# Moving weight and activation tiles by multiples of 32 bytes in a float32 decoder trunk

## The chip, the cores and the metric

The kernel runs on one core of a Trainium2 chip. The metric is device time in microseconds (us), lower is better. A core has five engines that run side by side, each with its own instruction queue: TensorE (PE; the load of its stationary operand is listed apart as PEld), VectorE (DVE), ScalarE (ACT), GpSimd (POOL) and SyncE (SP), which here only starts transfers. Two things are read by TensorE out of the on-chip memory (SBUF) at the same time: the **moving** operand of the matmul that runs, and the **stationary** operand ("weights" in the profile, LDWEIGHTS) of the matmul that comes next.

## The reference

A batch of one, 256 positions, width 2048, two layers, everything in float32:

```python
for l in range(DEPTH):                      # 2
    h = rms_norm(x, norm1_g[l])
    z = h @ w_in[l]                         # 2048 x 5120
    q, k, v, gu, gv = split(z)              # 1024 columns each
    attn = dilated_attention(rotary(q), rotary(k), v)
    gm = chunked_gmlp(gelu(gu), gelu(gv), ...)
    x = x + concat(attn, gm) @ w_out[l]     # 2048 x 2048
    h2 = rms_norm(x, norm2_g[l])
    x = x + square(relu(h2 @ w_up[l])) @ w_down[l]   # 2048 x 8192, 8192 x 2048
return rms_norm(x, final_g)
```

Nearly all the work is the four products with a weight matrix.

## The kernel before

**Float32 out of three products.** Every weight element and every activation is split into a high part (rounded to the type float32r, in which a matmul runs in one pass) and a low part (the rest). A product is then three matmuls: weight high by activation high, weight low by activation high, weight high by activation low.

**Weight steps.** The weights are cut into 736 blocks of 128 x 1024 elements (`Sub`), 512 KB each, in the order of use. One *step* is the work on one block: SP loads it into a buffer `raw` (L106), ACT copies it rounded into `hi` (`high`, L113), DVE subtracts into `lo` (`low`, L121), and PE runs the matmuls. The three tiles come from rings of buffers, `raw` 6, `hi` 7, `lo` 6; a ring's next buffer is free when its last readers are done. The number of the step (`self.i`) fixes the buffer.

**Two kinds of step.** In a `transposed` step (672 of 736) the weight block is the stationary operand: for each of two column blocks and four row blocks there are three matmuls of 128 x 256, one each on L263 (weight high), L265 (weight low) and L267 (weight high), so 24 in a step, with the activation as the moving operand. That is `hs`, the normed input, in 352 of the steps (q, k, gu and the MLP's up product); in the other 320 it is a tile `half` (1024 features, high and low; `new_half`), which holds the attention's output, the gating's output, or one eighth of the MLP's inner activations: two for `w_out` (`mix_a`, `mix_g`), eight for `w_down` (`hid[e]`), each layer. There are two `half` buffers, used in turn. In a `natural` step (64: v and gv) the activation `hs` is stationary and the weight block moves: 12 matmuls of 128 x 512, on L286 (high), L287 (low), L288 (high).

**Order.** The program is written out by one loop over the steps. At step `done` it emits `high` up to six blocks ahead, `low` up to five ahead, then the loads as far as the `raw` ring allows, then the matmuls; small pieces of attention and gating are put between the steps by a list with due times. In the MLP 16 up steps (one eighth) and 16 down steps take turns.

```python
ahead = min(2 + max(done - 10, 0) // 2, LO_BUFS - 2)
high_to(done + 2 + ahead)
low_to(done + 1 + ahead)
load_to(n_low[0] + RAW_BUFS)
mm()
```

**Where the tiles lie.** Tiles are laid one after another in each partition of SBUF, in units of 32 bytes. `hs` begins at a multiple of 64 bytes, and so does every 256-column piece of it. Behind it stands `warm`, one element, which takes 32 bytes; `raw`, `hi` and `lo` follow (4,096 bytes each), further on `half` (16,384 bytes each). All of these therefore begin 32 bytes past a multiple of 64, and so does each 128-column piece that a matmul reads of them. Below, a start is called *even* (a multiple of 64) or *odd* (32 past one).

Of the kernel before, what the change touches and what calls it, by code (L numbers as in the profile page):

```python
# [22 lines left out]
F32R = mybir.dt.float32r  # L23
# [5 lines left out]
P = 128  # L29
D = 2048  # L30
S = 256
DEPTH = 2
KC = D // P
NH = 8
# [9 lines left out]
BRANCHES = ((128, 1), (512, 4), (2048, 16))  # L44
NEG = -1.0e30

RAW_BUFS = 6
HI_BUFS = 7
LO_BUFS = 6
BUDGET = 1.2  # L50
# [22 lines left out]
def trunk(ctx: ExitStack, tc: tile.TileContext, layout, xT, consts, gains, w, b_sp, w_sp, out):  # L73
# [3 lines left out]
    wp = ctx.enter_context(tc.tile_pool(name="wp", bufs=1))  # L77
    tp = ctx.enter_context(tc.tile_pool(name="tp", bufs=1))
# [5 lines left out]
    def t32(name, shape, bufs=1, tag=None):  # L84
        return tp.tile([P, *shape], F32, name=name, tag=tag or name, bufs=bufs)
# [8 lines left out]
    class Sub:  # L94
# [7 lines left out]
        def load(self, parts):  # L102
            self.raw = wp.tile([P, 1024], F32, name="raw", tag="raw", bufs=RAW_BUFS)
            m = 1024 // parts
            for j in range(parts):
                nc.sync.dma_start(self.raw[:, j * m:(j + 1) * m], w[self.i][:, j * m:(j + 1) * m])  # L106

        def high(self, parts):
            self.h = wp.tile([P, 1024], F32R, name="hi", tag="hi", bufs=HI_BUFS)
            self.hi = self.h.rearrange("p (k n) -> p k n", n=self.n)  # L110
            m = 1024 // parts
            for j in range(parts):
                act.activation(self.h[:, j * m:(j + 1) * m], self.raw[:, j * m:(j + 1) * m], AF.Copy)  # L113

        def low(self, parts):
            lo = wp.tile([P, 1024], F32R, name="lo", tag="lo", bufs=LO_BUFS)
            self.lo = lo.rearrange("p (k n) -> p k n", n=self.n)
            m = 1024 // parts
            for j in range(parts):
                r = slice(j * m, (j + 1) * m)  # L120
                vec.tensor_tensor(lo[:, r], self.raw[:, r], self.h[:, r].bitcast(F32), op=OP.subtract)  # L121
# [176 lines left out]
    def from_tiles(tiles, n):  # L298
        return lambda k: tiles[k // n][0][:, k % n, :, :]

    def new_half(cell):
        cell[0] = tp.tile([P, NH, 2, S], F32R, name="half", tag="half", bufs=2)

    def gelu(z, u, then):

# [12 lines left out]
    def pair(ps):  # L318
        return ps.rearrange("p (a b) -> p a b", a=2)

    def update(norm, c, ps, final, last):

        alone = last and c == KC - 2
        for j in range(2) if alone else [slice(0, 2)]:
            xj = x[:, c + j, :] if alone else x[:, c:c + 2, :]
            vec.tensor_tensor(xj, xj, pair(ps)[:, j, :], op=OP.add)  # L326
        if final:
            if not last:
                norm.chunks(c)
            norm.square(c, alone)  # L330
            if last:
                norm.gain(c)

    def layer(l, n1, n2, n3, last):
# [104 lines left out]
        def values(j, pts):  # L439
            ps = aux_bank()  # L440
            vt = par["vt"]
            for h in range(2):
                c = (2 * j + h) * P
                pe.matmul(ps[:, h * S:(h + 1) * S], lhsT=vt[:, 0, c:c + P], rhs=pts[h][:, 0:S], start=(h == 0),  # L444
                          stop=False, skip_group_check=True)
                pe.matmul(ps[:, h * S + P:(h + 1) * S], lhsT=vt[:, 1, c:c + P], rhs=pts[h][:, S:3 * P], start=False,  # L446
                          stop=True, skip_group_check=True)
            if mix_a[0] is None:
                new_half(mix_a)
            to_half(mix_a[0], 2 * j, ps.rearrange("p (a b) -> p a b", a=2))  # L450
            par["heads"] += 1

        def to_half(t, c, src):
            act.activation(t[:, c:c + 2, 0, :], src, AF.Copy)  # L454
            vec.tensor_tensor(t[:, c:c + 2, 1, :], src, t[:, c:c + 2, 0, :].bitcast(F32), op=OP.subtract)  # L455
# [61 lines left out]
        def gate(g0, u, ps):  # L517
            sp = t32("sp", [2, S], tag="cross", bufs=2)
            for h in range(2):
                g = g0 + h  # L520
                vec.scalar_tensor_tensor(sp[:, h, :].rearrange("p (a b) -> p a b", a=2),
                                         ps[:, h * S:(h + 1) * S].rearrange("p (a b) -> p a b", a=2),
                                         lnb[:, l, 0, g:g + 1],
                                         par["spb"][:, g, None, :].to_broadcast([P, 2, P]),
                                         op0=OP.mult, op1=OP.add)
            vec.tensor_tensor(u, u, sp, op=OP.mult)
            if mix_g[0] is None:
                new_half(mix_g)
            to_half(mix_g[0], g0, u)
# [21 lines left out]
        hid = [[None] for _ in range(8)]  # L551

        def after_up(e):
            def f(c, ps):
                if hid[e][0] is None:
                    new_half(hid[e])
                z = t32("mz", [2, S], tag="tmpA")
                vec.tensor_tensor(z, pair(ps), n2.R[:, None, :].to_broadcast([P, 2, S]), op=OP.mult)  # L558
                vec.scalar_tensor_tensor(z, z, 0.0, z, op0=OP.max, op1=OP.mult)  # L559
                to_half(hid[e][0], c // P, z)  # L560
            return f

        base = len(steps)
        for e in range(9):
            if e < 8:
                transposed("w_up", l, 0, KC, e * 1024, 1024, from_hs, after_up(e))
            if e:
                transposed("w_down", l, (e - 1) * 1024, 8, 0, D, from_tiles([hid[e - 1]], NH),
                           lambda c, ps, e=e: update(n3, c // P, ps, e == 8, last))
# [19 lines left out]
    def load_to(n, parts=1):  # L589
        while n_load[0] < min(n, len(subs)):  # L590
            c = 2 * n_load[0]
            if c < KC:
                nc.sync.dma_start(x[:, c:c + 2, :], xv[:, c:c + 2, :])
            subs[n_load[0]].load(parts)
            n_load[0] += 1
# [6 lines left out]
    def low_to(n, parts=1):  # L602
        while n_low[0] < min(n, len(subs)):
            subs[n_low[0]].low(parts)
            n_low[0] += 1
# [4 lines left out]
    act.activation(warm, ones[:, 0:1], AF.Tanh)  # L610
    for i in range(RAW_BUFS):
        load_to(i + 1, 2 if i == 0 else 1)
# [6 lines left out]
    for n, (wt, mm, after) in enumerate(steps):  # L619
# [3 lines left out]
        else:  # L623
# [5 lines left out]
# [3 lines that stand above are left out]
# [9 lines left out]
    n = norms[-1]  # L641
# [42 lines left out]
```

## Time and profile before

| | |
|---|---|
| median of 2 runs | 2117.82 us (2117.58 to 2118.06) |
| profiled execution | 2117.06 us, of which the span of instructions is 2115.0 us |
| granted TensorE clock | 0.997 of full speed |
| PE / DVE / ACT / POOL busy | 2097.5 / 1254.7 / 929.9 / 63.2 us |
| transfers | 395.36 MB, mean 187 GB/s |
| an up step (moving `hs`) against a down step (moving `half`) | 340 against 355 matmuls touch a stretch of 40 us |

A group's row gives line, engine, operation, the tiles written and read, their shape and the count, then busy time and the mean time of one. A matmul's own time (about 280 ns) is longer than the distance from its start to the next one's (about 115 ns), since the array works on several in a row; what the span is made of is the distance between starts. In the order rows below, a name in brackets after "waits" is a counter that the instruction waits for: DMAHW of a transfer, DVE or Activation of those engines.

### The profile page before, as it was taken

The page shows a single profiled execution, that of the slowest core. Times are in us where ns is not written, and L with a number is a line of the kernel's source. Part 1 is how long each engine was busy: PE and PEld are TensorE (multiplying, and loading weights), DVE is VectorE, ACT ScalarE, POOL GpSimd, SP SyncE. Part 2 cuts the span into 40 slices and gives each one's busy share as a digit, 9 for nine tenths or more (in the row PEclk, how much of TensorE's full clock was granted, in tenths as well). Part 3 has the DMA queues.
Part 4 walks back from the last instruction along what each step waited for, and adds up shares of the span by engine and source line. Part 5 has one row for each costly group of instructions (what it writes and reads, how often), then busy time and mean ns, then how long its engine had stood idle before and what let it go on. Part 6 is the DMA issues. An engine that isn't in the chain of part 4 may idle for free.

```text
span 2115.0 us, 40168 instructions
## 1 busy us (share of the span) xinstructions
PE 2097.5 (99%) x17212; PEld 2057.2 (97%) x17212; DVE 1254.7 (59%) x1502; ACT 929.9 (44%) x1128; POOL 63.2 (3%) x90
## 2 busy tenths in 40 slices
PE   8999999999999999999999999999999999999997
PEld 7998999999999999999989989999999999999997
DVE  7566766555555555555755666665565555555555
ACT  6555444344333433433545554543443334434333
POOL 0002300000000000000000032000000000000000
PEclk9999999999999999999999999999999999999998
DMA  8545555555555556556564455555655655555552
GB/s 306 183 160 169 180 192 180 196 192 178 189 200 188 192 180 200 191 183 198 188 211 157 164 180 176 195 177 198 200 180 180 199 191 200 181 187 192 182 201 84
DMA packets 111523, 395.36 MB, mean 187 GB/s; under 512 B 12272, under 2 KB 16368, under 8 KB 111344
## 3 DMA queue, kind: packets, MB, share of 16 engines
q1 hardware_dynamic: 110480, 390.12, 54.7%
q8 instruction: 134, 2.20, 0.4%
q10 hardware_dynamic: 864, 2.68, 0.3%
q14 instruction: 45, 0.37, 0.1%
HBM read 390.65 MB, written 2.10 MB: 186 GB/s over the span
## 4 chain that ended last, share of the span: by engine, by line
PE 99%; DVE 0%; DMA 0%; ACT 0%; issue 0%; DVEq 0%; ACTq 0%
PE acc L263 29%; PE acc L265 29%; PE acc L267 29%; PE acc L286 3%; PE acc L287 3%; PE acc L288 3%; PE aux L500 0%; PE aux L444 0%; PE aux L404 0%; PE aux L433 0%; DVE x L646 0%; PE aux L201 0%; PE aux L407 0%; PE aux L446 0%; PE aux L354 0%; PE aux L208 0%
## 5 line engine op out<-in xcount | busy, mean ns | idle before, releaser
L113 ACT ACTIVATE hi<-raw 128x1024 fp32r<-128x1024 f32 (+1 forms) x737 | 754.7, 1053 | 473.6 <-PE acc L267 379.2
L121 DVE TENSOR_TENSOR lo<-raw,hi 128x1024 fp32r<-128x1024 f32 (+1 forms) x737 | 864.3, 1218 | 58.8 <-ACT hi L113 26.6
L263 PE MATMUL acc<-hs,hi 128*128 128x256 f32 x2816 | 793.8, 282 | 0.0
L267 PE MATMUL acc<-hs,hi 128*128 128x256 f32 x2816 | 791.1, 281 | 0.0
L265 PE MATMUL acc<-hs,lo 128*128 128x256 f32 x2816 | 791.0, 281 | 0.0
L263 PE MATMUL acc<-half,hi 128*128 128x256 f32 x2560 | 707.1, 276 | 0.0
L265 PE MATMUL acc<-half,lo 128*128 128x256 f32 x2560 | 706.8, 276 | 0.0
L267 PE MATMUL acc<-half,hi 128*128 128x256 f32 x2560 | 706.7, 276 | 0.0
L265 PEld LDWEIGHTS acc<-hs,lo 128*128 128x128 f32 x2816 | 530.7, 188 | 0.4 <-issue 0.2
L263 PEld LDWEIGHTS acc<-hs,hi 128*128 128x128 f32 x2816 | 530.6, 188 | 0.4 <-issue 0.2
L267 PEld LDWEIGHTS acc<-hs,hi 128*128 128x128 f32 x2816 | 530.6, 188 | 0.0
L267 PEld LDWEIGHTS acc<-half,hi 128*128 128x128 f32 x2560 | 480.7, 188 | 0.0
L263 PEld LDWEIGHTS acc<-half,hi 128*128 128x128 f32 x2560 | 480.7, 188 | 0.0
L265 PEld LDWEIGHTS acc<-half,lo 128*128 128x128 f32 x2560 | 480.6, 188 | 0.0
L326 DVE TENSOR_TENSOR x<-x,acc 128x512 f32<-128x512 f32 (+1 forms) x152 | 99.5, 659 | 319.6 <-PE acc L267 319.6
L454 ACT ACTIVATE half<-mz 128x512 fp32r<-128x512 f32 x64 | 40.5, 632 | 379.7 <-DVE mz L559 379.7
L558 DVE TENSOR_TENSOR mz<-acc,nR 128x512 f32<-128x512 f32 x64 | 44.3, 692 | 258.0 <-PE acc L267 258.0
L286 PE MATMUL acc<-hi,hs 128*128 128x512 f32 x256 | 103.3, 404 | 5.4 <-ACT hi L113 5.4
L287 PE MATMUL acc<-lo,hs 128*128 128x512 f32 x256 | 102.1, 399 | 0.0
L288 PE MATMUL acc<-hi,hs 128*128 128x512 f32 x256 | 101.7, 397 | 0.0
L176 ACT ACTIVATE hs<-x,cols 128x256 fp32r<-128x256 f32 x64 | 29.1, 502 | 96.4 <-DVE x L326 94.8
L455 DVE TENSOR_TENSOR half<-mz,half 128x512 fp32r<-128x512 f32 x64 | 44.4, 693 | 44.7 <-ACT half L454 44.7
(90 smaller groups left out, 674.7 us busy)
## 6 DMA issues: line engine op xcount, KB each, us to landing
raw<-in_w SPq DMA_DIRECT2D x735, 512.0 KB, 4.4
x<-in_xT SPq DMA_DIRECT2D x8, 256.0 KB, 7.0
out<-x SPq DMA_DIRECT2D x8, 256.0 KB, 3.0
spb<-in_b_sp ACTq DMA_DIRECT2D x2, 512.0 KB, 7.9
wsp<-in_w_sp ACTq DMA_DIRECT2D x2, 512.0 KB, 9.3
raw<-in_w SPq DMA_DIRECT2D x2, 256.0 KB, 3.9
con<-in_consts ACTq DMA_DIRECT2D x1, 512.0 KB, 6.8
cols<-in_gains ACTq DMA_DIRECT2D x1, 56.0 KB, 2.8
```

The costliest lines, as they stand in the source:

```text
L113: act.activation(self.h[:, j * m:(j + 1) * m], self.raw[:, j * m:(j + 1) * m], AF.Copy)
L121: vec.tensor_tensor(lo[:, r], self.raw[:, r], self.h[:, r].bitcast(F32), op=OP.subtract)
L263: pe.matmul(o, lhsT=hi, rhs=xs[:, 0, :], start=(k0 + k == 0 and cb == 0), stop=False, skip_group_check=True)
L265: pe.matmul(o, lhsT=wt.lo[:, k, cb * P:(cb + 1) * P], rhs=xs[:, 0, :], start=False, stop=False, skip_group_check=True)
L267: pe.matmul(o, lhsT=hi, rhs=xs[:, 1, :], start=False, stop=last, skip_group_check=True)
L286: pe.matmul(ps, lhsT=xh, rhs=hi, start=(k0 + k == 0), stop=False)
L287: pe.matmul(ps, lhsT=xh, rhs=lo, start=False, stop=False)
L288: pe.matmul(ps, lhsT=xl, rhs=hi, start=False, stop=(k0 + k == KC - 1))
L326: vec.tensor_tensor(xj, xj, pair(ps)[:, j, :], op=OP.add)
L454: act.activation(t[:, c:c + 2, 0, :], src, AF.Copy)
L455: vec.tensor_tensor(t[:, c:c + 2, 1, :], src, t[:, c:c + 2, 0, :].bitcast(F32), op=OP.subtract)
L558: vec.tensor_tensor(z, pair(ps), n2.R[:, None, :].to_broadcast([P, 2, S]), op=OP.mult)
```

## The change

Three edits. `hi` and `lo` tiles become 96 bytes longer (4,192 bytes), and the block begins 0, 32, 64 or 96 bytes into its tile, by the number of the step modulo 4. `half` tiles become 480 bytes longer (16,864 bytes), and eighth `e` of layer `l` begins 32 x (8l + e) bytes into its tile; `mix_a` and `mix_g` begin at its start. The `raw` ring has 5 buffers in place of 6.

```diff
+PAD = 8
-RAW_BUFS = 6
+RAW_BUFS = 5
@@ Sub.high
-            self.h = wp.tile([P, 1024], F32R, name="hi", tag="hi", bufs=HI_BUFS)
+            o = PAD * (self.i % 4)
+            self.h = wp.tile([P, 1024 + 3 * PAD], F32R, name="hi", tag="hi", bufs=HI_BUFS)[:, o:o + 1024]
@@ Sub.low
-            lo = wp.tile([P, 1024], F32R, name="lo", tag="lo", bufs=LO_BUFS)
+            o = PAD * (self.i % 4)
+            lo = wp.tile([P, 1024 + 3 * PAD], F32R, name="lo", tag="lo", bufs=LO_BUFS)[:, o:o + 1024]
@@
-    def new_half(cell):
-        cell[0] = tp.tile([P, NH, 2, S], F32R, name="half", tag="half", bufs=2)
+    def new_half(cell, shift=0):
+        n = NH * 2 * S
+        t = tp.tile([P, n + 15 * PAD], F32R, name="half", tag="half", bufs=2)
+        cell[0] = t[:, shift * PAD:shift * PAD + n].rearrange("p (a b c) -> p a b c", a=NH, b=2)
@@ after_up
-                    new_half(hid[e])
+                    new_half(hid[e], 8 * l + e)
```

**What starts where after it.** 4,192 bytes are 65.5 x 64, so the start of each following buffer of a ring changes between odd and even, and the shift of the step changes it once more each step. In the `lo` ring of 6 the two cancel: every `lo` starts even. In the `hi` ring of 7 they cancel for seven steps, and the ring's return to its first buffer then turns them over: `hi` starts odd for seven steps, even for seven, and so on. 16,864 bytes are 263.5 x 64, and with two buffers and a shift that grows by one with each eighth the two cancel again: every `hid[e]` and `mix_a` start even, `mix_g` alone starts odd. `hs` stays where it was, even.

No engine's instructions change place. On SP a load that found its buffer free at the start now waits for one. SP's queue before, from its eleventh row (x is the layer input, fetched in eight pieces; the number behind `raw` tells tiles apart):

```order
10 L106 DMA raw_95<-in_w 128x1024 [waits DMAHW3_49]
11 L593 DMA x_75<-in_xT 128x2x256 [waits DMAHW4_49]
12 L106 DMA raw_98<-in_w 128x1024 [waits DMAHW5_49]
13 L593 DMA x_75<-in_xT 128x2x256 [waits DMAHW6_49]
14 L106 DMA raw_129<-in_w 128x1024 [waits DMAHW7_49,DVE_49]
15 L593 DMA x_75<-in_xT 128x2x256 [waits DMAHW0_49]
```

SP's queue at the same place in the changed program:

```order
10 L107 DMA raw_95<-in_w 128x1024 [waits DMAHW3_49]
11 L598 DMA x_75<-in_xT 128x2x256 [waits DMAHW4_49]
12 L107 DMA raw_126<-in_w 128x1024 [waits DMAHW5_49,DVE_49]
13 L598 DMA x_75<-in_xT 128x2x256 [waits DMAHW6_49]
14 L107 DMA raw_129<-in_w 128x1024 [waits DMAHW7_49,DVE_49]
15 L598 DMA x_75<-in_xT 128x2x256 [waits DMAHW0_49]
```

The sixth block's load (row 12) now waits for DVE, which has to be done with the first block; from there on each load waits for the block five before it, where it was six.

## The prediction

> **What bounds the kernel now.** First the engines' shares, the granted clock and the chain of waits on the page, then the list of all that PE ever waited for:
>
> ```profile
> PE 2097.5 (99%) x17212; PEld 2057.2 (97%) x17212; DVE 1254.7 (59%) x1502; ACT 929.9 (44%) x1128; POOL 63.2 (3%) x90
> PEclk9999999999999999999999999999999999999998
> PE 99%; DVE 0%; DMA 0%; ACT 0%; issue 0%; DVEq 0%; ACTq 0%
> ```
> ```profile
> PE acc L286 <- ACT hi L113: 5.4, 1, 5.4
> PE aux L208 <- DVE nr L227: 2.4, 1, 2.4
> PE aux L201 <- ACT nsq L184: 0.2, 1, 0.2
> ```
>
> PE is busy in 99% of the span, at the full clock, and waits 8.0 us in all, 5.4 of them for the first weight block. So nothing that feeds PE sets the time; only the pace of the matmuls can. Next, the groups of matmuls, and two stretches of equal length, one in an up piece (moving `hs`), one in the down piece behind it (moving `half`); the columns are the busy time and count of PE, PEld, DVE, ACT and POOL, then clock and transfers:
>
> ```profile
> L265 PE MATMUL acc<-hs,lo 128*128 128x256 f32 x2816 | 791.0, 281 | 0.0
> L265 PE MATMUL acc<-half,lo 128*128 128x256 f32 x2560 | 706.8, 276 | 0.0
> ```
> ```profile
> 568.00:608.00 40.00, 40.00 (x340) 40.00 (x339) 22.56 (x24) 15.76 (x17) 0.00 (x0) 1.00 0.54 184
> 612.00:652.00 40.00, 40.00 (x355) 40.00 (x354) 23.92 (x25) 17.66 (x18) 0.00 (x0) 1.00 0.58 187
> ```
>
> The same instruction of the same shape is not equally fast. In each window about 2.5 of the counted matmuls started ahead of it (280 ns long, one every 115), so the distance between starts is 40,000/337.5 = 118.5 ns with `hs` and 40,000/352.5 = 113.5 ns with `half`: **5.0 ns** more with `hs`, though DVE, ACT and the transfers are a little busier in the other window. So those are not what slows it. One line of each stretch, with shortest, median and longest time:
>
> ```profile
> L265 PE MATMUL acc<-hs,lo x114: 277/280/285, 567.8 to 607.9; 128*128 128x256 f32 x114
> ```
> ```profile
> L265 PE MATMUL acc<-half,lo x119: 276/276/276, 611.8 to 651.9; 128*128 128x256 f32 x119
> ```
>
> With `half` every one takes 276 ns; with `hs` they scatter from 277 to 285. A constant against a scatter looks like two streams that meet, and the difference between the two kinds that stands in the code is where the operands start. Stationary `hi` and `lo` start odd in both; moving `hs` starts even, moving `half` odd. I take as theory: **the matmul that runs and the weight load beside it disturb each other when one starts even and the other odd** ("out of phase"), and not when both start alike ("in phase"). Before, all 8,446 such pairs with `hs` are out of phase and all but one of the 7,679 with `half` are in phase (a pair is a matmul and the load of the weights of the next).
>
> **The raw ring** costs nothing. Who held up the users of `raw`, how long a load takes to land, and what the loads wait for:
>
> ```profile
>   DMA raw<-in_w: 4.0, 10
> DMA to landing us min/median/max: 3.0/4.4/8.6
> ```
> ```profile
> SPq L106 <- DVE lo L121: 1717.3, 714, 8.6
> ```
>
> A step takes 24 x 118.5 ns = 2.84 us at most. A load is written into the program five steps ahead of the copy of its block by ACT, which makes 14.2 us against a longest landing of 8.6; with one buffer less it is 11.4 us, still over 8.6. Behind a waiting load on SP's queue stand only loads, and at the start the pieces of x; the cover is that ACT's copies stand up to six blocks ahead of PE and DVE's subtractions up to five. If that cover fails, the ten holds at the start are where: 4.0 us in all, so I bound this at 0 to +4 us and take 0.
>
> **Even or odd, counted over** the starts in the two built programs. In the changed program `lo` is always even, `hi` odd for seven steps and even for seven, `half` even but for `mix_g`, `hs` even. In a transposed step with `hi` even all 24 pairs are in phase; with `hi` odd only the pair "high weight runs, low is loaded" is, and the two others of each three are not. By pairs:
> - `hs`: 2,845 stay out of phase, 5,601 come into phase. In steps: 174 wholly in phase, 178 with two thirds out.
> - `half`: 2,805 out of phase, against 1. In steps: 145 wholly in, 143 with two thirds out, 16 (`mix_g`, `hi` even) wholly out, 16 (`mix_g`, `hi` odd) with one third out.
> - natural steps (the weights move, `hs` is loaded): 764 out before, 242 after. 34 steps wholly in, 30 mixed.
>
> The price of a transposed pair is the 5.0 ns. For a natural pair no row shows it in phase; their starts, and the nearest row, four matmuls of 256 columns in full float32, whose own time (379 ns) is the nearest to theirs (395):
>
> ```profile
> 16.04 0.40 PE L286 MATMUL acc<-hi,hs 128*128 128x512 f32 x1
> ...
> 18.84 0.40 PE L286 MATMUL acc<-hi,hs 128*128 128x512 f32 x1
> ```
> ```profile
> 83.88 1.03 PE L404 MATMUL aux<-k,q 128*128 128x256 f32 x4
> ```
> ```profile
> L404 PE MATMUL aux<-k,q x32: 377/379/380, 83.9 to 1208.4; 128*128 128x256 f32 x32
> ```
> ```profile
> L287 PE MATMUL acc<-lo,hs x34: 393/395/397, 16.3 to 39.4; 128*128 128x512 f32 x34
> ```
>
> From 16.04 to 18.84 lie twelve natural matmuls, 233 ns each; the four on L404, both operands odd, lie (1,030 - 379)/3 = 217 ns apart. So a natural pair out of phase costs between 0 and 16 ns; I take 16, since both the distance and the own time point to it.
>
> What a mixed step costs is not in the trace, and it is the largest unknown. If each pair pays for itself (**end A**), the change is -5,601 x 5.0 = -28.0 for `hs`, +2,804 x 5.0 = +14.0 for `half`, -522 x 16 = -8.4 for the natural steps: **-22.4 us**. But a disturbed stream seems to need time to settle. This is the first step on `half` after the `hs` steps of the gating, all its pairs in phase:
>
> ```profile
> 252.39 0.29 PE L263 MATMUL acc<-half,hi 128*128 128x256 f32 x1
> ...
> 255.10 0.28 PE L267 MATMUL acc<-half,hi 128*128 128x256 f32 x1
> ```
>
> 23 distances in 2.71 us, 118 ns each: slow from end to end, on addresses that run at 113.5 later. So a mixed step, whose good pairs come singly, may stay slow throughout (**end B**): then `hs` gains only its 174 clean steps, 174 x 24 x 5.0 = -20.9; `half` loses 175 steps, +21.0; the natural steps gain 34 x 12 x 16 = -6.5: **-6.4 us**. (With nothing from the natural steps B is +0.1.) No row is nearer to one end than to the other, so I take the middle: **-14.4 us**.
>
> The shifted starts also move what ACT writes and DVE reads and writes. A copy or subtraction that grew or shrank by some per cent would stay hidden, since ACT and DVE are busy 44% and 59% of the time and PE waited 2.6 us in all after the start. The aux matmuls of attention and gating (316 records) keep their starts relative to each other, but for a few against constants: 0.
>
> Sum: profiled execution 2117.06 - 14.4 = 2102.7; the median of the runs lies 0.8 above that execution, so **2103 us**.
>
> [...]
>
> **The rivals.**
> 1. *Nothing changes, 2118.* The difference between `hs` and `half` comes from something the offsets leave alone, such as the region in which the tiles lie, or the state in which a stream happens to have settled. For it: the slow step at 252.39 on good addresses. Against it: `hs` scatters over all its 2,816 matmuls of a line while `half` is constant, and neither window's engines explain it. Chance 0.12. [...]
> 2. *The period is 128 bytes, slower.* Before, `half` and the weights lay 64 bytes apart modulo 128, `hs` 32; after it, half of the pairs that I call in phase lie 0 apart, and the trace has no such pair. If two streams that start in the same place of 128 disturb each other as much as those 32 apart, only 2,784 pairs with `hs`, 2,444 with `half` and 247 natural ones are good. By pairs: `hs` -2,782 x 5.0 = -13.9, `half` +5,235 x 5.0 = +26.2, natural -243 x 16 = -3.9: +8.4 us, 2126. By steps, in which only 12 of the `half` steps, 10 of the `hs` steps and 6 natural ones are clean: +308 x 0.12 - 10 x 0.12 - 6 x 0.19 = +34.6, 2152. Middle 2139. It decides where more than about half of these pairs are bad. Chance 0.15.
> 3. *The moving operand's own start counts, slower.* If a moving row that starts even is slow whatever the weights do, `hs` stays slow and 6,911 of the `half` pairs join it: +34.6 us, 2152. For it: `hs` is even and slow, `half` odd and fast, and nothing in the transposed steps separates this from my theory. Against it: the natural steps move odd rows, and are the ones with 16 ns too much. Chance 0.09.
> 4. *One good pair in three is enough to settle.* Then the mixed steps are as fast as the clean ones: `hs` -352 x 0.12 = -42.2, `half` +16 x 0.12 = +1.9, natural -64 x 12 x 16 ns = -12.3: -52.6, 2065. The step at 252.39 speaks against it. Chance 0.06.
>
> **How the numbers follow.** My forecast (A to B, 2095 to 2111, with some room for the natural steps) has 0.53; 0.05 is left for sums that none of these gives. The range reaches from somewhat under A to the upper part of rival 2: 2090 to 2150, which leaves out rivals 3 and 4 and a little of 2. Within 2% is 2075 to 2160, about what a measurement of this kernel tells from no change: forecast, rivals 1 to 3 and most of the rest lie there. Faster by more is rival 4 alone, which lies just beyond 2075: 0.05. Slower by more are rivals 2 and 3 with a price above 5.0 ns: 0.05. That leaves 0.90 within.
>
> **What would show it.** If I am right, the `hs` groups fall from 281 ns toward 278 to 279, the `half` groups rise from 276 to 278 or so, L286 to L288 fall; in a clean step every matmul takes 276 ns, with `hs` as with `half`, and the slow steps come in runs of seven. Rival 2 shows as clean steps with scatter, rival 3 as `hs` still at 281 in every step and `half` at 281 too, rival 1 as 281 and 276 unchanged. PE's waits should stay near 8 us; if they grow, the raw ring was not free. I am wrong if clean steps are not at 276, or if a step's pace does not follow `hi`'s start.

## The result, and the profile after

The changed kernel takes **2150.49 us** (median of 2 runs, 2150.41 to 2150.57) against 2117.82 before: 1.0154 times as long, interval 1.0111 to 1.0198. It became slower by 33 us; 2103 was forecast, with a range up to 2150.

The engines' shares and what PE waited for, in the changed kernel:

```profile
PE 2130.9 (99%) x17212; PEld 2092.4 (97%) x17212; DVE 1254.8 (58%) x1502; ACT 929.6 (43%) x1128; POOL 66.4 (3%) x90
PEclk9999999999999999999999999999999999999998
```
```profile
PE acc L289 <- ACT hi L115: 5.4, 1, 5.4
PE aux L211 <- DVE nr L230: 2.4, 1, 2.4
PE aux L204 <- ACT nsq L187: 0.2, 1, 0.2
```

PE has 33.4 us more of busy time, for the same number of instructions, at the same clock (0.997), with the same waits to a tenth of a microsecond. DVE and ACT are unchanged. So the matmuls themselves run at a slower pace. Which of them, the groups tell (L263, L265, L267 before are L266, L268, L270 now; L287 is L290):

```profile
L268 PE MATMUL acc<-hs,lo 128*128 128x256 f32 x2816 | 789.9, 280 | 0.0
L266 PE MATMUL acc<-half,hi 128*128 128x256 f32 x2560 | 718.6, 281 | 0.0
L270 PE MATMUL acc<-half,hi 128*128 128x256 f32 x2560 | 718.6, 281 | 0.0
L268 PE MATMUL acc<-half,lo 128*128 128x256 f32 x2560 | 717.8, 280 | 0.0
L290 PE MATMUL acc<-lo,hs 128*128 128x512 f32 x256 | 101.4, 396 | 0.0
```

The lines of them before that the prediction did not show:

```profile
L263 PE MATMUL acc<-half,hi 128*128 128x256 f32 x2560 | 707.1, 276 | 0.0
L267 PE MATMUL acc<-half,hi 128*128 128x256 f32 x2560 | 706.7, 276 | 0.0
L287 PE MATMUL acc<-lo,hs 128*128 128x512 f32 x256 | 102.1, 399 | 0.0
```

The three lines on `half` take 11.5, 11.9 and 11.0 us more, 34.4 in all; the line on `hs` 1.1 us less (791.0 before), the natural line 0.7 less. Everything that the change cost, it cost on the down products and `w_out`; what it was to gain on `hs` did not come. The distances between starts, added up over the whole trace, say the same: +35.4 us on `half`, -0.5 on `hs`, -1.5 on the natural steps, 33.4 in all. The windows of an up piece and of the down piece behind it:

```profile
578.00:618.00 40.00, 40.00 (x339) 40.00 (x339) 21.06 (x24) 14.00 (x16) 0.00 (x0) 1.00 0.56 187
620.00:660.00 40.00, 40.00 (x343) 40.00 (x342) 23.04 (x24) 16.49 (x17) 0.00 (x0) 1.00 0.57 187
```

Before they were 340 and 355 matmuls. Inside this down piece, three steps in a row and then the next ones, by shortest, median and longest time of a matmul:

```profile
L268 PE MATMUL acc<-half,lo x24: 276/276/276, 637.0 to 644.8; 128*128 128x256 f32 x24
```
```profile
L268 PE MATMUL acc<-half,lo x23: 274/280/285, 647.0 to 654.8; 128*128 128x256 f32 x23
```

Fast steps exist, so the pace does follow the step. But by the distances between starts in the whole trace only 36 of the 672 transposed steps run below 115 ns per matmul once under way (from the ninth on), where the prediction's theory has 319 clean ones (174 with `hs`, 145 with `half`).

### The profile page after: what moved, and what is told of

Read it like the earlier page. It is cut to its first block, busy times and chain, and to the rows that moved or that the text cites. A ratio compares the mean times of both kernels' runs of the same rounds, so it can differ in the third digit from the quotient of the medians.

```text
span 2148.3 us, 40170 instructions
## 1 busy us (share of the span) xinstructions
PE 2130.9 (99%) x17212; PEld 2092.4 (97%) x17212; DVE 1254.8 (58%) x1502; ACT 929.6 (43%) x1128; POOL 66.4 (3%) x90
## 4 chain that ended last, share of the span: by engine, by line
PE 99%; DVE 0%; DMA 0%; ACT 0%; issue 0%; DVEq 0%; ACTq 0%
PE acc L266 30%; PE acc L270 30%; PE acc L268 30%; PE acc L289 3%; PE acc L290 3%; PE acc L291 3%; PE aux L505 0%; PE aux L449 0%; PE aux L409 0%; PE aux L438 0%; DVE x L651 0%; PE aux L204 0%; PE aux L412 0%; PE aux L451 0%; PE aux L359 0%; PE aux L211 0%
## 5 line engine op out<-in xcount | busy, mean ns | idle before, releaser
L266 PE MATMUL acc<-hs,hi 128*128 128x256 f32 x2816 | 793.8, 282 | 0.0
L270 PE MATMUL acc<-hs,hi 128*128 128x256 f32 x2816 | 791.3, 281 | 0.0
L268 PE MATMUL acc<-hs,lo 128*128 128x256 f32 x2816 | 789.9, 280 | 0.0
L266 PE MATMUL acc<-half,hi 128*128 128x256 f32 x2560 | 718.6, 281 | 0.0
L270 PE MATMUL acc<-half,hi 128*128 128x256 f32 x2560 | 718.6, 281 | 0.0
L268 PE MATMUL acc<-half,lo 128*128 128x256 f32 x2560 | 717.8, 280 | 0.0
L266 PEld LDWEIGHTS acc<-hs,hi 128*128 128x128 f32 x2816 | 530.9, 189 | 0.4 <-issue 0.2
L268 PEld LDWEIGHTS acc<-hs,lo 128*128 128x128 f32 x2816 | 530.6, 188 | 0.4 <-issue 0.2
L270 PEld LDWEIGHTS acc<-hs,hi 128*128 128x128 f32 x2816 | 530.0, 188 | 0.0
L268 PEld LDWEIGHTS acc<-half,lo 128*128 128x128 f32 x2560 | 482.2, 188 | 0.0
L266 PEld LDWEIGHTS acc<-half,hi 128*128 128x128 f32 x2560 | 482.2, 188 | 0.0
L270 PEld LDWEIGHTS acc<-half,hi 128*128 128x128 f32 x2560 | 482.0, 188 | 0.0
L290 PE MATMUL acc<-lo,hs 128*128 128x512 f32 x256 | 101.4, 396 | 0.0
L179 ACT ACTIVATE hs<-x,cols 128x256 fp32r<-128x256 f32 x64 | 29.0, 501 | 102.1 <-DVE x L331 100.6
```

The costliest lines, as they stand in the source:

```text
L266: pe.matmul(o, lhsT=hi, rhs=xs[:, 0, :], start=(k0 + k == 0 and cb == 0), stop=False, skip_group_check=True)
L268: pe.matmul(o, lhsT=wt.lo[:, k, cb * P:(cb + 1) * P], rhs=xs[:, 0, :], start=False, stop=False, skip_group_check=True)
L270: pe.matmul(o, lhsT=hi, rhs=xs[:, 1, :], start=False, stop=last, skip_group_check=True)
L290: pe.matmul(ps, lhsT=xh, rhs=lo, start=False, stop=False)
```

## The experiments

Three theories were open. *Period of 64*: the prediction's, only even against odd counts. *Period of 128*: rival 2, operands have to stand 64 bytes apart modulo 128. *Own start*: rival 3, a moving operand that starts even is slow. "Distance" below is the start of the weights that are loaded less the start of the operand that moves. All edits are to the kernel before or to the first experiment; runs of the kernel before beside them had medians between 2117.29 and 2117.58 us. Where a time stands without an interval, it is of a single run.

**All distances 64 modulo 128.** The one-element tile behind `hs` is made longer:

```diff
-    warm = cp.tile([P, 1], F32, name="warm")
+    warm = cp.tile([P, 16], F32, name="warm")
-    act.activation(warm, ones[:, 0:1], AF.Tanh)
+    act.activation(warm[:, 0:1], ones[:, 0:1], AF.Tanh)
```

> The kernel before, with the one-element tile behind hs made 64 bytes long in place of 32, so that everything behind it moves by 32 bytes. Now the weights stand 64 bytes from the moving or stationary hs modulo 128 (32 before), and 64 from half, as before. Period of 128, 64 apart is good: every pair is good, hs falls from 118.3 to 113.4 ns per matmul, 8,448 x 5 ns = -42 us, and the natural steps gain 0 to 12 us: 2063 to 2076. Period of 64 (the theory of the prediction): the same. The moving operand's own start decides (even is slow): hs stays even and slow, half becomes even and slow: 2118 + 7,680 x 5 ns = 2156. Neither, the region or the history of the stream decides: 2118.

Measured: **2075.58 us**, ratio 0.9803 (0.9787 to 0.982). Its groups on the low weights:

```profile
L265 PE MATMUL acc<-hs,lo 128*128 128x256 f32 x2816 | 778.6, 276 | 0.0
L265 PE MATMUL acc<-half,lo 128*128 128x256 f32 x2560 | 706.7, 276 | 0.0
```

`hs`, still even, now runs at 276 ns, and `half`, even now as well, stays there. Own start falls: it gave 2156. The phase between two operands is worth 42 us, by 32 bytes of SBUF.

**All distances 0 modulo 128.** `warm` has 32 elements, and `half` a tile 128 bytes longer of which the first 64 are skipped:

```diff
+    warm = cp.tile([P, 32], F32, name="warm")
+        n = NH * 2 * S
+        t = tp.tile([P, n + 32], F32R, name="half", tag="half", bufs=2)
+        cell[0] = t[:, 16:16 + n].rearrange("p (a b c) -> p a b c", a=NH, b=2)
```

> The kernel before, with gaps of 96 bytes behind hs and 64 bytes ahead of the parts of half that are used, so that moving and stationary operands all stand 0 bytes apart modulo 128. Period of 64: 0 is as good as 64, all pairs fast, 2063 to 2076. Period of 128 with 64 alone good: hs no better than before (118 to 119 ns), half slow too, 2118 + 7,680 x 5 to 6 ns = 2156 to 2168. The moving operand's own start: hs even, half even, 2156.

Measured: **2165.41 us**, ratio 1.0227 (1.0207 to 1.0248).

```profile
L265 PE MATMUL acc<-hs,lo 128*128 128x256 f32 x2816 | 792.7, 281 | 0.0
L265 PE MATMUL acc<-half,lo 128*128 128x256 f32 x2560 | 722.4, 282 | 0.0
```

Modulo 256 these distances are 128 for `hs` and, since the longer tile moves the second buffer by 128, 0 and 128 by turns for `half`. Every operand starts even, every pair is in phase by the prediction's theory, and it is the slowest arrangement so far. **The period of 64 falls here.** From this kernel to the one above it, the same instructions differ by 90 us through their addresses alone.

**Everything 32 bytes further.** `con`, ahead of `hs`, is 8 elements longer; all distances stay:

```diff
-    con = cp.tile([P, 1024], F32, name="con")
+    con = cp.tile([P, 1024 + 8], F32, name="con")[:, 0:1024]
```

> The kernel before, with 32 bytes more in front of hs, so that all of hs, raw, hi, lo and half move together: distances as before, every start changes between even and odd. Distance decides (period 64 or 128): 2118, hs at 281 ns and half at 276 as before. The moving operand's own start decides: hs, odd now, falls to 276 ns (-42 us) and half, even now, rises to 281 (+38 us).

Measured: 2117.92 us, the groups unmoved:

```profile
L265 PE MATMUL acc<-hs,lo 128*128 128x256 f32 x2816 | 791.0, 281 | 0.0
L265 PE MATMUL acc<-half,lo 128*128 128x256 f32 x2560 | 706.8, 276 | 0.0
```

The distance decides, not the operand's own start.

**Five raw buffers alone** (`RAW_BUFS = 5`, nothing else).

> The kernel before with 5 raw buffers in place of 6 and nothing else (4,096 bytes less, so no distance changes modulo 128). The ring is free: 2118, within 2 us, PE's waits near 8 us. If the ring carries part of the 33 us: up to 2150, with PE waiting for hi or lo.

Measured: 2117.32 us, ratio 1.0001 (0.9992 to 1.001). The ring is free.

**The edit of `half` alone** (`new_half` and its call in `after_up` as in the change).

> The kernel before with the edit of half alone (longer tile, shifted by eighth; hi, lo and raw as before). By the addresses, half now stands 64 from the weights in mix_a and in four of the eight eighths (two in a row, then two not), 0 in the other four, 96 in mix_g; hs stays at 32. Period of 128: 3,839 half pairs become slow, at the 5.0 ns of 32 or the 6 ns that the run with 0 everywhere gave: +19 to +23 us, 2136 to 2141, and the down pieces come fast, fast, slow, slow. Period of 64: only mix_g gets slow, +4 us, 2121.

Measured: 2144.76 us, 4 more than the upper end. Why, the windows of the down pieces of eighths 0 to 5 show (count of PE's matmuls in 40 us):

```profile
437.00:477.00 40.00, 40.00 (x355) 1.00 0.61 196
526.00:566.00 40.00, 40.00 (x355) 1.00 0.62 196
616.00:656.00 40.00, 40.00 (x336) 1.00 0.59 186
708.00:748.00 40.00, 40.00 (x335) 1.00 0.58 189
799.00:839.00 40.00, 40.00 (x342) 1.00 0.60 191
890.00:930.00 40.00, 40.00 (x342) 1.00 0.59 195
```

Fast and slow come by twos as a period of 128 has it, but the third pair, 64 apart modulo 128 like the first, runs at 117.8 ns (40,000/339.5, by the prediction's allowance of 2.5). The difference: the first pair's distance is 64 modulo 256, the third's 192. So 128 is not the whole period, or those pieces were caught in a slow pace.

**The edit of `hi` and `lo` alone** (as in the change).

> The kernel before with the edit of hi and lo alone (longer tiles, shifted by step; half and raw as before). Period of 128 with 64 alone good: 2,784 of 8,448 hs pairs and 2,543 of 7,679 half pairs at 64, nearly all of them in steps that also hold others. Each pair pays for itself: hs -14 us, half +26 us, 2129. A step is slow as a whole unless it is clean: about the time of the changed kernel, 2150.

Measured: 2149.58 us, within 1 us of the full change. This edit alone costs what all of them cost: with it, the edit of `half`, which alone cost 27 us, adds 1.

**Distances 96 and 32.** `warm` has 24 elements, `half` is shifted by 32 bytes in a tile 128 bytes longer.

```diff
+    warm = cp.tile([P, 24], F32, name="warm")
+        t = tp.tile([P, n + 32], F32R, name="half", tag="half", bufs=2)
+        cell[0] = t[:, 8:8 + n].rearrange("p (a b c) -> p a b c", a=NH, b=2)
```

> The kernel before with other gaps: hs stands 96 from the weights modulo 128 everywhere, half 32. It fills the table of distances. Period of 128 with 64 alone good: hs slow as before, half slow as hs was at 32 (118.3 ns), 2117 + 7,680 x 5 = 2155. If 32 were slow for another reason with hs than the distance: half stays at 113.4 and the time at 2117.

Measured: 2159.02 us; L265 takes 280 ns with `hs`, 282 with `half`. Neither is good: `hs` is as slow at 96 as it was at 32, and `half`, fast at 64, is slow at 32 in one buffer and, its tile being 128 bytes longer, at 160 in the other.

**`hs` 16 bytes into a longer tile.** The first experiment with `hs` 16 bytes into a tile 128 bytes longer:

```diff
+    hs = cp.tile([P, KC * 2 * S + 32], F32R, name="hs")[:, 4:4 + KC * 2 * S].rearrange("p (a b c) -> p a b c", a=KC, b=2)
```

> The kernel with everything 64 apart, but hs 16 bytes further, so that it stands 48 from the weights; half stays at 64. If a neighbourhood of 64 is good: 2076, hs at 113.8 ns. If it has to be 64 to within 16 bytes: hs slow as at 32, 118 ns, 2117. Half way: the distance works gradually.

Measured: 2131.46 us, worse than any theory had it. The edit does not do what was expected of it: the longer tile also moves the weights by 128 bytes. Between `hs` and the weights now lie 112 bytes of its own tile and the 64 of `warm`, 176 in all, which is 48 modulo 128 but not modulo 256. `hs` is slow there (281 ns), 16 bytes from 192, a distance that a run below finds slow as well; how narrow the good place at 64 is, this run does not show. Most of the 14 us above the kernel before lie on `half`, whose distance is the good one throughout: 710.4 us on L265 in place of 706.8, 10.6 us over its three lines. Windows of the down pieces of eighths 0 and 1, and of `w_out`:

```profile
441.00:481.00 40.00, 40.00 (x342) 1.00 0.59 187
530.00:570.00 40.00, 40.00 (x355) 1.00 0.56 186
300.00:340.00 40.00, 40.00 (x342) 1.00 0.50 171
```

Eighth 1 is fast, eighth 0 and `w_out` are slow on the same distance. In eighth 0 every matmul takes the same time:

```profile
L265 PE MATMUL acc<-half,lo x114: 281/281/281, 441.0 to 480.9; 128*128 128x256 f32 x114
```

Its pace, 40,000/339.5 = 117.8 ns, is that of the step at 252.39 that the prediction quoted: a stream can settle in a second, slower and equally regular pace on a good distance, and keep it for a whole piece.

**One bad pair of three.** The first experiment with each `lo` 64 bytes into a longer tile, so that `lo` stands 0 modulo 128 from the moving operand and `hi` 64:

```diff
+            lo = wp.tile([P, 1024 + 32], F32R, name="lo", tag="lo", bufs=LO_BUFS)[:, 16:16 + 1024]
```

> The kernel with everything 64 apart, but each lo 64 bytes further into a longer tile, so that lo alone stands 0 from hs and from half. In every transposed step one pair of three is bad: the one in which a high weight runs and the low one is loaded. This prices a mixed step. Each pair pays for itself (end A of the prediction): 2076 + 16,128/3 x 5 to 6 ns = 2103 to 2108. One bad pair of three keeps the whole step slow (end B): 2076 + 16,128 x 5 to 6 ns = 2156 to 2172.

Measured: **2165.43 us**, as much as with every pair at 0.

```profile
L265 PE MATMUL acc<-hs,lo 128*128 128x256 f32 x2816 | 791.3, 281 | 0.0
L265 PE MATMUL acc<-half,lo 128*128 128x256 f32 x2560 | 719.3, 281 | 0.0
```

End B: one pair of three at 0 modulo 128 takes the pace from the whole step; these rows are matmuls of which the next load (a high block) is at the good distance.

**256 bytes more behind `hs`.** The first experiment with `warm` of 80 elements.

> The kernel with everything 64 apart modulo 128, with 256 bytes more behind hs: the distance from hs to the weights is 320 modulo 512, as it is for half, in place of 64. If only the 128 matter: 2076 within 2 us, with the same share of hs steps that stay at 118 ns in the attention part. If a longer period plays a part: those steps go (2070 to 2072) or become more.

Measured: 2075.47 us, ratio 0.9803 (0.9787 to 0.982), against 2075.58 in the first experiment; L265 takes 277 ns with `hs` (276 there) and 276 with `half`, as there. 256 bytes change nothing in the time.

**All distances 192 modulo 256.** The first experiment with `warm` of 48 elements and `half` 128 bytes into a tile 256 bytes longer:

```diff
+    warm = cp.tile([P, 16 + 32], F32, name="warm")
+        t = tp.tile([P, n + 64], F32R, name="half", tag="half", bufs=2)
+        cell[0] = t[:, 32:32 + n].rearrange("p (a b c) -> p a b c", a=NH, b=2)
```

> The kernel with everything 64 apart modulo 128, moved so that all distances are 192 modulo 256 in place of 64. In the run with the edit of half alone, the two eighths at 64 modulo 256 ran at 113.4 ns and the two at 192 at 117.8, all 16 steps of each, though both are 64 modulo 128. Period of 128, and those two eighths only kept the slow pace in which they were entered: 2076. Period of 256, 192 is not a good distance: 117.8 ns everywhere, 2076 + 16,128 x 4.4 = 2147.

Measured: **2145.98 us**.

```profile
L265 PE MATMUL acc<-hs,lo 128*128 128x256 f32 x2816 | 787.7, 280 | 0.0
L265 PE MATMUL acc<-half,lo 128*128 128x256 f32 x2560 | 716.3, 280 | 0.0
```

128 bytes further, the kernel takes 70 us more than in the first experiment, while 256 bytes more changed nothing. **By these runs the period is 256**: as the one distance of all pairs, 64 is good and 192 is not. (Four `hs` steps of the 672 did run at 113 ns, so 192 does not exclude the fast pace; the stream hardly ever finds it.)

**`lo` at 192, `hi` at 64.** Counted over the starts in the built program, which no view of a run shows, 20 steps of the changed kernel had `hi` at 64 and `lo` at 192 modulo 256, and none of them was slow. This is the first experiment with that pairing everywhere, and five raw buffers for the room:

```diff
-RAW_BUFS = 6
+RAW_BUFS = 5
+            lo = wp.tile([P, 1024 + 64], F32R, name="lo", tag="lo", bufs=LO_BUFS)[:, 32:32 + 1024]
```

> The kernel with everything 64 apart, with each lo 128 bytes further into a longer tile (192 modulo 256; hi stays at 64) and 5 raw buffers, for room. In the changed kernel the clean steps with hi at 64 and lo at 192 ran at 113.3 to 114 ns without exception, those with both at 64 at 113.4 or at 117.8. If that pairing gets out of the slow pace by itself: the 50-odd hs steps at 118 ns in the attention part go, 2076 - 5 = 2071. If only the 128 matter: 2076 within 1 us.

Measured: **2073.18 us** (2072.03 to 2074.11), ratio 0.9788 (0.9775 to 0.9802). In the first experiment 34 transposed steps, 32 of them on `hs` and nearly all in the attention and gating part, had settled in the slow pace, by the distances between starts; the row below, from its trace, shows a stretch of them. Here, by the distances between starts, there are none. At 24 x 4.4 ns a step they are worth 3.6 us; the medians differ by 2.4, and the intervals of the two ratios overlap, so the gain in time is likely but not settled:

```profile
L265 PE MATMUL acc<-hs,lo x21: 281/281/281, 240.9 to 247.9; 128*128 128x256 f32 x21
```

So one pair of three at 192 does no harm beside two at 64, where one at 0 modulo 128 slowed them all and 192 throughout was slow: what a distance costs depends on the other distances in the step. This kernel and the first experiment beat both kernels, by 44 and 42 us against before.

## Why the prediction was wrong

- **What bounds the kernel: right.** Only the pace of the matmuls moved the time; PE's waits, 8.0 us before, were 8.0 in the changed kernel and 7.9 to 8.8 in the experiments, and DVE and ACT were busy for 1254.8 and 929.6 us in the changed kernel against 1254.7 and 929.9.
- **The raw ring at 0: right**, 2117.32 against 2117.29.
- **That the distance between the two operands decides: right.** Everything moved by 32 bytes gave 2117.92; distances changed by 32 gave 2075.58.
- **That even against odd is all of it: wrong, and this is the step that failed.** "5,601 come into phase" counted as good what stands 0, 64, 128 and 192 apart. As the one distance of a step only 64 modulo 256 was good, a quarter of them. With everything at 0 modulo 128 the kernel took 2165, not 2063 to 2076. The trace of before held two distances for the transposed steps, one good and one bad, and any period that separates them fitted; I took the shortest.
- **The mixed step: end B, not the middle.** One pair of three at 0 modulo 128 gave 2165.43. With B alone the forecast would have been 2111, still on the wrong side, so this is not what turned the sign. The row at 252.39 spoke for B, and I gave it no more than half.
- **The sum, term by term.** `hs`: -20.9 to -28.0 forecast, -0.9 measured over its three lines, since only 15 of 352 `hs` steps became fast. `half`: +14.0 to +21.0 forecast, +34.4 measured, since all 320 steps had been at the good distance and 21 stayed fast. Natural steps: -6.5 to -8.4 forecast, -1.4 measured over their three lines; even in the first experiment their busy time on L287 came to 100.8 us in place of 102.1, and the distance between their starts to 228.4 ns in place of 233.3. The 16 ns were read off a row of full float32 matmuls, of which the trace has two records for each one in the program (32 on L404 for 16), where float32r has one (2,816 on L265 for 352 x 8); they were not to be had at any distance tried.
- **The rivals.** Rival 2 by steps gave 2152.4, within 2 us, for a reason that was half right: every constant distance tried that is not 64 modulo 128 was slow, but 64 modulo 128 is not enough. That its time came so near is partly luck, since its good steps were counted by the wrong period. Rival 1 falls as a whole with the first experiment, though the state in which a stream has settled, which it named, does exist (117.8 ns at 64). Rival 3 falls with the shift by 32, rival 4 with the run with `lo` at 0. The range ended at 2150 because I cut off rival 2's upper part; the time lies 0.5 us beyond it.

Why did the change undo what was there? The kernel before had, by the lengths of its tiles, one constant distance per operand, and that of `half` was the good one. Offsets that change from step to step spread the pairs over all eight multiples of 32. Of these 64 alone was fast as a constant distance (224 was not tried, 160 only by turns with 32), and two good pairs of three did not save a step in the run with `lo` at 0. Only 36 of 672 steps came out fast. That it is the distances, and not the changing from step to step as such, is argued from these runs; a run with offsets that change by multiples of 256 would separate the two, and none was made.

## What to carry to other kernels

Where TensorE is the bound, compare the own times of one matmul shape over its different operands: a difference of 5 ns between two operands can come from the addresses, and here one tile made 32 bytes longer was worth 2%. A constant time is no proof of the fast pace: with all distances at 192 every L265 of an up piece took 280 ns. Choose one distance between the moving and the stationary operand and keep it for every step, by making ring buffers a multiple of 256 bytes long, rather than spreading over many; in this kernel 64 modulo 256 was the one to choose. When a tile is lengthened to shift its contents, work out anew what lies behind it. A trace that shows two distances doesn't give the period; a run with another distance does, and it costs one line.

## What the runs showed of the hardware that was not expected

Pace of the transposed matmuls (128 x 256, float32r) against the distance of their operands, as the mean own time of L265 in runs where the distance is constant:

| distance, bytes modulo 256 | own time, ns | run |
|---|---|---|
| 64 | 276 | before (`half`), first experiment (both) |
| 192 | 280 | all at 192 (both) |
| 128 | 281 | all at 0 (`hs`) |
| 0 and 128 by turns | 282 | all at 0 (`half`) |
| 32 | 281 | before (`hs`) |
| 32 and 160 by turns | 282 | 96 and 32 (`half`) |
| 96 | 280 | 96 and 32 (`hs`) |
| 176 | 281 | `hs` 16 bytes into a longer tile |

At the good distance there are two stable paces on the same addresses, 113.4 and 117.8 ns between starts; the run with `hs` at 176 lost 10.6 us in `half` steps of the good distance. In the first experiment a pace held until something else came between: by the distances between starts, two steps of one kind that follow each other directly have the same pace in all 609 cases, and of 29 places where matmuls of attention or gating stand between two such steps, the pace changes at 20. What in them changes it is not shown. With `half` at 0 modulo 128 the weight load took longer too, 192 ns in place of 187 to 188; with `lo` alone at 0 the median of the loads on L265 stayed at 188 in an up piece. From the edit of `half` alone, eighth 0 and eighth 2 (0 modulo 128):

```profile
L265 PEld LDWEIGHTS acc<-half,lo x118: 187/188/188, 437.1 to 476.9; 128*128 128x128 f32 x118
```
```profile
L265 PEld LDWEIGHTS acc<-half,lo x112: 192/192/192, 616.0 to 655.9; 128*128 128x128 f32 x112
```

In the slow pace at 64, L265's loads took 192 ns in the first experiment's steps at 241 us, and 187 to 188 in eighth 0 of the run with `hs` at 176, with matmuls of 281 ns in both.

What stays open: by what the distance acts on the pace, why 64 is good and 192 is not, how far from 64 the good place reaches, why a pair at 192 does no harm beside two at 64, which of the two paces a stream settles in at 64, and whether a distance exists at which the natural steps lose their 16 ns. None of these was tried further.
